# Recurrence mixer: two kinds of products interleaved, the gate chain cut into steps, order written out for each engine

## The chip, the cores and the metric

The kernel runs on one core of a Trainium2 chip. The metric is the device time of one execution in microseconds (us). The engines are named as the profile names them: PE is TensorE (PEld its weight loads), DVE is VectorE, ACT is ScalarE, POOL is GpSimd, SP is SyncE, whose queue issues most transfers.

## The reference, cut to what matters

The program is a stack of mixers and feed-forward networks over 512 tokens of width 1024, in eight stages. The change is in the third, the recurrence mixer (`rglru_mixer`), 1280 wide in ten heads of 128:

```python
proj = u @ w_in + b_in
ybr = jax.nn.gelu(proj[..., :LRU_WIDTH])
xbr = causal_dwconv(proj[..., LRU_WIDTH:], conv_w, conv_b)      # 4 taps
xh = xbr.reshape(bsz, s, LRU_HEADS, LRU_BLOCK)
gx = jax.nn.sigmoid(einsum('bshi,hij->bshj', xh, w_gx) + b_gx)
ga = jax.nn.sigmoid(einsum('bshi,hij->bshj', xh, w_ga) + b_ga)
log_a = LRU_C * ga * jax.nn.log_sigmoid(lam)
a_t = jnp.exp(log_a)
b_t = jnp.sqrt(-jnp.expm1(2.0 * log_a)) * gx * xbr
_, h = lax.associative_scan(_linear_combine, (a_t, b_t), axis=1)   # h_t = a_t h_(t-1) + b_t
out = (h * ybr) @ w_out + b_out
```

So a head has a branch product with a convolution behind it, two gate products of 128 by 128, a scan along the tokens, and a gelu product that multiplies the scan's result. `log_sigmoid(lam)` depends on the parameters alone.

## The kernel before, in words

Channels lie on the partitions, the 512 tokens (`T`) along a row. All matmuls are split in two parts of a value: a high part, rounded, and a low part, the remainder. A product of the input with a chunk of 128 output channels (`proj`) is 8 blocks of the contraction, each three matmuls of 512 columns (`mm3`: high by high, L429; low activation, L430; low weight, L431), so 24 in all, in one PSUM bank of the ring `mm`, which has three banks.

**Weights.** All weight chunks lie in one array in the order in which the program wants them. SP loads them two chunks at a time into `raw`. A chunk is split as two halves of 512 columns (`Weights._half`): the high part by a cast (`wh<-raw`), then the low part by a subtraction on VectorE (`wl<-raw`, L295). A plan says where the cast runs: "av" puts it on ScalarE (L292), "vv" on VectorE (L294). The plan is ("av",) in all stages but this one, where halves alternate by `PLAN = {"lru": ("av", "vv")}`. `W.next` splits ahead of need by `look`, two halves; `W.reserve` and `W.more` put halves into other tiles of the stage and split them earlier still.

**The stage.** At its entry `lru` computes what depends on the parameters alone: softplus of `lam` (17 steps on VectorE, one exp on ScalarE), the vector for the convolution's first columns (`less`) and halved gate biases (`hb`). Then a small scheduler, `Flow`, runs generators by priority and writes instructions in the order in which they yield. The generator `dense` makes the ten branch products b0 to b9 first. Behind each stand the convolution (`conv`: a first step on ScalarE, L690, three on VectorE, L693, and a correction) and the split of its result (`xb`). For each pair of heads it spawns `gates` with a delay: four gate products of three matmuls, four tanh from PSUM (L1051), two tanh (L1058), two exps (L1063), two square roots (L1066), and for each head a scan step of three VectorE instructions on `th`, `gt` and `h` (L1067 to L1070). The ten gelu products g0 to g9 follow: gelu on ScalarE, times `h`, split into `hs`. They come in groups of 4, 2 and 4, and each group's down product (`down`, 8 steps of one PSUM bank each, summed by VectorE into `acc`) is made behind the products of the next group. The last down product belongs to `stage_end`, with the norms of the next stage's input. Exp, square root and gelu (tanh shares gelu's and exp's) want different sets of ScalarE's function tables; where a set is wanted that isn't there, the program holds an `ACT_TABLE_LOAD`.

**What sets the order.** Within one engine a tile scheduler issues what the program writes, in its written order but for what its own priorities move forward; between engines semaphores hold.

Of the kernel before, what the change touches and what calls it, by code (L numbers as in the profile page):

```python
# [16 lines left out]
P = 128  # L17
# [68 lines left out]
G_MLA = _groups(4, 2, 2)  # L86
G_FF = {FF1: _groups(*(4,) * 8), FF2: _groups(*(4,) * 5, 2)}
# [74 lines left out]
def weights(i, used):  # L162
# [12 lines left out]
    lin = _up(w, list(range(10, 20)) + list(range(10)))  # L175
# [168 lines left out]
def build(tc, nc, aps, at, stages):  # L344
# [4 lines left out]
    with ExitStack() as st:  # L349
# [380 lines left out]
        def ssd(pl, ent, pre, fin):  # L730
# [213 lines left out]
            def last_homes():  # L944
                def two(a, b, bufs):
                    return lambda: tuple(pl.tile([P, T], F32R, name=n, tag=t, bufs=m)
                                         for n, t, m in (("wh", a, bufs[0]), ("wl", b, bufs[1])))

                def both():
                    t = pl.tile([P, 2, T], F32R, name="w2", tag="xdt", bufs=2)  # L950
# [54 lines left out]


        def lru(pl, ent, pre, fin):
            acc = [pl.tile([P, 1024], F32, name=f"acc{q}") for q in range(4)]
            NH = 10
            xs = ent.xs  # L1010
            flow = Flow()
            pre = list(pre)
            held_b = [None]


            few_ = pl.tile([P, 5 * NH], F32, name="few_")
# [6 lines left out]
            less = pl.tile([P, NH, 3], F32, name="less")  # L1023
# [9 lines left out]
            hseq, held, done = {}, [None], [0]  # L1033

            def unit():
# [6 lines left out]
            def gates(pair, xb, xbs):  # L1042
                hold = []
                for h in pair:
                    if h % 4 == 0:
                        held[0] = W.next("lg")
                    for n in range(2):
                        ps = mmps("ax")
                        mm3(ps, held[0].blk(2 * (h % 4) + n), xbs[h], True, True)
                        gt = tmp("gt")  # L1050
                        A.activation(gt, ps, AF.Tanh, scale=0.5, bias=hb[:, NH * n + h:NH * n + h + 1])  # L1051
                        hold.append(gt)
                gx, ga = hold[0::2], hold[1::2]

                ths, ats = [], []
                for n, h in enumerate(pair):
                    th = tmp("th")
                    A.activation(th, ga[n], AF.Tanh, scale=psp[:, h:h + 1], bias=psp[:, h:h + 1])  # L1058
                    V.scalar_tensor_tensor(gx[n], gx[n], 1.0, xb[h], op0=ALU.add, op1=ALU.mult)
                    ths.append(th)  # L1060
                for n, h in enumerate(pair):
                    a_ = tmp("at")
                    A.activation(a_, ga[n], AF.Exp, scale=nsp[:, h:h + 1], bias=nsp[:, h:h + 1])  # L1063
                    ats.append(a_)
                for n, h in enumerate(pair):
                    A.activation(ths[n], ths[n], AF.Sqrt, scale=0.25)  # L1066
                    V.scalar_tensor_tensor(ths[n], ats[n], 1.0, ths[n], op0=ALU.add, op1=ALU.mult)  # L1067
                    tt(gx[n], gx[n], ths[n])
                    hh = pl.tile([P, T], F32, name=f"h{h}")
                    V.tensor_tensor_scan(hh, ats[n], gx[n], initial=0.0, op0=ALU.mult, op1=ALU.add)  # L1070
                    hseq[h] = hh
                done[0] += 1
                yield 2.6, 0.0

            def dense():
                for p in range(0, NH, 2):
                    xb, xbs = {}, {}
                    yield 0.0, 0.0, lambda: done[0] >= p // 2 - 1
                    for h in (p, p + 1):
                        ps = unit()  # L1080
                        o = conv("co", ps, 4, [vc("lcw", NH * t_ + h) for t_ in range(4)], lcb[:, h:h + 1])
                        tt(o[:, :3], o[:, :3], less[:, h], ALU.subtract)
                        xb[h], xbs[h] = o, split(pl, o, "xb", bufs=4)
                        yield 5.2, 0.0
                    flow.spawn(gates((p, p + 1), xb, xbs), 0, 11.0)
                prev = None
                for q, grp in enumerate(G_LRU):
                    hs = []
                    if q == 1:
                        held_b[0] = row(5)  # L1090
                    for h in grp:
                        ps = unit()
                        t = tmp("t")
                        A.activation(t, ps, AF.Gelu_apprx_tanh, bias=vc("lbin", h))
                        yield 5.2, 0.0, lambda: h in hseq
                        tt(t, t, hseq[h])
                        hs.append(split(pl, t, "hs", bufs=7))
                    if q == 2:
                        W.reserve(len(W.used) + len(prev), last_homes())
                    if prev is not None:  # L1100
                        for d in down("lout", prev, acc, bias_first if q == 1 else None):
                            if q == 2:
                                W.more()
                            yield d
                    prev = hs
                held[0] = prev

            def last_homes():
                def hp(h):
                    return lambda: tuple(pl.tile([P, T], F32R, name=n, tag=f"h{h + e}")  # L1110
                                         for e, n in enumerate(("wh", "wl")))

                def xb():
                    return tuple(pl.tile([P, T], F32R, name="w" + n, tag="xb" + n, bufs=4) for n in "hl")
                return [xb, xb, xb, xb, hp(0), hp(2), hp(4)]

            def bias_first(a, ps, h):
                tt(a, ps, held_b[0][h], ALU.add)
            flow.spawn(dense(), 3)
            flow.run()  # L1120
            return fin("lout", held[0], acc, 1)
# [674 lines left out]
        def ffn(pl, ent, pre, fin, n, side=None):  # L1796
# [39 lines left out]
            def last_homes():  # L1836
                def one(k):
                    def f():
                        if n == 1 and k < 2:
                            t = pl.tile([P, 2, T], F32R, name="w2", tag=("HD", "W_")[k], bufs=1)  # L1840
                        else:
                            t = pl.tile([P, 2, T], F32R, name=f"w2{k}")
# [28 lines left out]
        PLAN = {"lru": ("av", "vv")}  # L1871
# [62 lines left out]
```

## Time and profile before

| | before |
|---|---|
| median of 3 runs (lowest, highest) | 2921.78 us (2921.23, 2925.98) |
| profiled execution | 2921.57 us, its span 2919.8 us |
| PE busy | 2849.1 us, 98% of the span |
| PEld busy | 2328.5 us, 80% |
| DVE busy | 1845.0 us, 63% |
| ACT busy | 1285.7 us, 44% |
| POOL busy | 314.3 us, 11% |
| mean granted clock of TensorE | 0.991 |
| instructions, bytes moved by DMA | 35383, 285.70 MB |

The table gives averages over eight stages with different loads. The recurrence stage's own products run from 1000.35 to 1165.12 us of the span. A row of the order views below gives the start in us, the length of one, the engine, the line, the operation with its output and inputs, and in brackets the idle time before it and whose result ended it; x4 is four in a row of the same kind, whose time is the sum. Granted clock is the share of full clock that TensorE was given.

### The profile page before, as it was taken

How to read it: one execution, taken by the hardware profiler on the slowest of the kernel's cores; microseconds unless marked ns; L12 is line 12 of the kernel's file. 1: busy time of each engine (PE TensorE's matmuls, PEld its weight loads, DVE VectorE, ACT ScalarE, POOL GpSimd, SP SyncE). 2: the span in 40 equal slices, each digit the busy share in tenths (PEclk: the TensorE clock that was granted, in tenths of full speed). 3: DMA queues.
4: the chain of work that ended last, by engine and by line, in shares of the span. 5: the costliest groups of instructions: out<-in, count | busy, mean ns of one | idle time of the engine just before them, and what ended most of it. 6: DMA issues, size and time to landing. Idle time of an engine off the chain costs nothing.

```text
span 2919.8 us, 35383 instructions
## 1 busy us (share of the span) xinstructions
PE 2849.1 (98%) x13528; PEld 2328.5 (80%) x13528; DVE 1845.0 (63%) x3001; ACT 1285.7 (44%) x2273; POOL 314.3 (11%) x458
## 2 busy tenths in 40 slices
PE   8999999999999989999999999999999999999998
PEld 7777778888888867888878878888888876788886
DVE  6887776556556777775766665655445566554454
ACT  5444346434334672643433354654333454443332
POOL 1233210000000000112233221100000000000000
PEclk9999999999999989999999999999999999999999
DMA  3212222222223123133333336522222221122222
GB/s 138 73 58 73 76 105 87 101 87 101 101 87 126 55 79 137 62 105 109 130 109 121 122 127 190 156 70 101 101 87 101 91 73 44 58 101 101 87 100 81
DMA packets 100184, 285.70 MB, mean 98 GB/s; under 512 B 19632, under 2 KB 28336, under 8 KB 99504
## 3 DMA queue, kind: packets, MB, share of 16 engines
q1 hardware_dynamic: 89376, 272.15, 26.8%
q10 hardware_dynamic: 10640, 11.30, 1.2%
q8 instruction: 106, 1.74, 0.2%
q14 instruction: 62, 0.51, 0.1%
HBM read 269.31 MB, written 14.12 MB: 97 GB/s over the span
## 4 chain that ended last, share of the span: by engine, by line
PE 76%; DVE 4%; ACT 3%; issue 1%; POOL 1%; DMA 0%; DVEq 0%; POOLq 0%; ACTq 0%
PE mm L429 16%; PE mm L430 16%; PE mm L431 16%; PE dn L561 6%; PE dn L560 6%; PE dn L562 6%; PE mm L562 1%; PE mm L560 1%; PE mm L561 1%; PE ax L1744 1%; PE ax L1766 1%; ACT sq L506 1%; DVE wl L295 1%; PE ax L1743 1%; DVE x L425 1%
## 5 line engine op out<-in xcount | busy, mean ns | idle before, releaser
L292 ACT CAST wh<-raw 128x512 fp32r<-128x512 f32 x889 | 548.9, 622 | 1135.3 <-PE mm L430 719.0
L429 PE MATMUL mm<-xh,wh 128*128 128x512 f32 (+1 forms) x2600 | 980.7, 379 | 21.3 <-DVE xl L549 11.8
L295 DVE TENSOR_TENSOR wl<-raw,wh 128x512 fp32r<-128x512 f32 x922 | 667.7, 731 | 511.1 <-ACT wh L292 495.0
L431 PE MATMUL mm<-xh,wl 128*128 128x512 f32 (+1 forms) x2600 | 977.9, 377 | 10.9 <-DVE wl L295 10.8
L430 PE MATMUL mm<-xl,wh 128*128 128x512 f32 (+1 forms) x2600 | 977.9, 377 | 1.3 <-DVE xl L549 0.9
L429 PEld LDWEIGHTS mm<-xh,wh 128*128 128x128 f32 x2600 | 491.5, 190 | 117.9 <-DVE xl L549 13.0
L431 PEld LDWEIGHTS mm<-xh,wl 128*128 128x128 f32 x2600 | 493.2, 190 | 100.9 <-DVE wl L295 12.8
L430 PEld LDWEIGHTS mm<-xl,wh 128*128 128x128 f32 x2600 | 493.2, 190 | 89.4 <-DVE xl L549 2.3
L560 PE MATMUL dn<-wh,hsh 128*128 128x512 f32 x816 | 321.1, 394 | 2.6 <-DVE acc L425 2.6
L561 PE MATMUL dn<-wl,hsh 128*128 128x512 f32 x816 | 322.2, 395 | 0.2 <-DVE wl L295 0.2
L562 PE MATMUL dn<-wh,hsl 128*128 128x512 f32 x816 | 317.5, 389 | 0.0
L514 POOL TENSOR_SCALAR rr<-ss 128x1 f32<-128x1 f32 x52 | 15.9, 306 | 1689.8 <-ACT sq L506 1688.8
L560 PEld LDWEIGHTS dn<-wh,hsh 128*128 128x128 f32 x816 | 153.4, 188 | 38.9 <-DVE acc L425 3.0
L562 PEld LDWEIGHTS dn<-wh,hsl 128*128 128x128 f32 x816 | 153.6, 188 | 34.3
L561 PEld LDWEIGHTS dn<-wl,hsh 128*128 128x128 f32 x816 | 153.8, 189 | 31.2 <-DVE wl L295 0.7
L693 DVE SCALAR_TENSOR_TENSOR ca<-mm,vec,ca 128x510 f32<-128x510 f32 x216 | 161.6, 748 | 11.8 <-ACT ca L690 8.2
L425 DVE TENSOR_TENSOR acc<-dn,acc 128x512 f32<-128x512 f32 x112 | 76.9, 687 | 88.5 <-PE dn L562 88.1
L425 DVE TENSOR_TENSOR x<-dn,x 128x512 f32<-128x512 f32 x96 | 66.0, 689 | 103.9 <-PE dn L562 103.9
L693 DVE SCALAR_TENSOR_TENSOR cb<-mm,vec,cb 128x510 f32<-128x510 f32 (+1 forms) x128 | 95.7, 748 | 10.7 <-ACT cb L690 8.7
L443 ACT CAST hsh<-act 128x512 fp32r<-128x512 f32 x108 | 67.2, 622 | 69.1 <-DVE act L425 69.0
L425 DVE TENSOR_TENSOR hsl<-act,hsh 128x512 fp32r<-128x512 f32 x108 | 79.8, 739 | 10.6 <-ACT hsh L443 2.7
L690 ACT ACTIVATE ca<-mm,vec 128x512 f32<-128x512 f32 x108 | 83.8, 776 | 5.6 <-PE mm L431 5.3
(504 smaller groups left out, 3191.3 us busy)
## 6 DMA issues: line engine op xcount, KB each, us to landing
raw<-w SPq DMA_DIRECT2D x233, 1024.0 KB, 4.8
sD<-s5t SPq DMA_DIRECT2D x4, 1024.0 KB, 6.9
row<-rows SPq DMA_DIRECT2D x12, 256.0 KB, 5.2
sR<-s5t SPq DMA_DIRECT2D x4, 768.0 KB, 4.3
x<-x SPq DMA_DIRECT2D x8, 256.0 KB, 5.1
xo<-x ACTq DMA_DIRECT2D x8, 256.0 KB, 4.8
s5t<-el ACTq DMA_DIRECT2D x8, 256.0 KB, 2.9
s5t<-HD ACTq DMA_DIRECT2D x4, 512.0 KB, 3.1
```

Of the source, the lines that this page charges most:

```text
L292: c.nc.scalar.copy(hi, r)
L295: (c.nc.gpsimd if e[1] == "g" else c.nc.vector).tensor_tensor(lo, r, hi.bitcast(F32), op=ALU.subtract)
L425: (eng or V).tensor_tensor(o, a, b, op=op)
L429: PE.matmul(ps, lhsT=wh, rhs=xh, start=first, stop=False)
L430: PE.matmul(ps, lhsT=wh, rhs=xl, start=False, stop=False)
L431: PE.matmul(ps, lhsT=wl, rhs=xh, start=False, stop=last)
L443: A.copy(hi, src)
L560: PE.matmul(ps, lhsT=hh[:, qs], rhs=wh, start=first, stop=False)
L561: PE.matmul(ps, lhsT=hh[:, qs], rhs=wl, start=False, stop=False)
L562: PE.matmul(ps, lhsT=hl[:, qs], rhs=wh, start=False, stop=last)
L690: A.activation(o, src, AF.Identity, scale=w[nt - 1], bias=b)
L693: V.scalar_tensor_tensor(o[:, d:], src[:, :T - d], w[j], o[:, d:], op0=ALU.mult, op1=ALU.add)
```

## The change

The stage is no longer run by `Flow`; it is written out.

- **Products interleaved.** `LRU_UNITS` lists branch (b) and gelu (g) products in the order b0 to b5, g0, g1, b6, b7, g2, g3, b8, b9, g4 to g9, and the weights are stored in that order.
- **The gate chain as steps.** A class `Gates` holds a pair of heads. `first` (a head's two gate products), `second` (its three tanh) and `third` (a VectorE product) are written into the code of a later product, one head for each product; `exps`, `roots` (two square roots, and then a preload of gelu's table set) and `scan` stand between products. The last pair's gate products stand inside the first down product.
- **Order fixed.** `in_order` adds, for PE, ACT, DVE and Pool, a dependence of each instruction on the one written before it on the same engine, so that the scheduler moves nothing.
- **Weights.** `PLAN` is empty: all casts run on ScalarE. In all, 33 casts leave VectorE for ScalarE. For three gate chunks the second half gets tiles of its own (`W.homes`).
- **Parameters.** Softplus, `less` and `hb` move into `lru_vectors`, which the feed-forward stage ahead calls at its fourth group; their tiles live in the pool `main`.
- **Tiles.** The convolution's output `cb` has four buffers, the scan's result `hq` four in place of ten tiles `h0` to `h9`, `hs` six for seven. The two transfers of the output bias stand at the stage's start and not at the second group.
- Table loads: 52 in the program where 46 stood, 16 where 11 stood in the recurrence stage. The renaming of `w2` to `wh2` in other stages changes nothing else.

```diff
+LRU_UNITS = [(u[0], int(u[1])) for u in
+             "b0 b1 b2 b3 b4 b5 g0 g1 b6 b7 g2 g3 b8 b9 g4 g5 g6 g7 g8 g9".split()]
...
-    lin = _up(w, list(range(10, 20)) + list(range(10)))
+    lin = _up(w, [10 * (b == "b") + h for b, h in LRU_UNITS])
...
+        class in_order:
+            def __enter__(self):
+                self.n = len(nc.cur_bb.bb.instructions)
+            def __exit__(self, *a):
+                last = {}
+                E = mybir.EngineType
+                for i in nc.cur_bb.bb.instructions[self.n:]:
+                    if i.engine not in (E.PE, E.Activation, E.DVE, E.Pool):
+                        continue
+                    if i.engine in last:
+                        tc.add_manual_dep(i, last[i.engine].name, mybir.DependencyInfo(
+                            mybir.DependencyClass.NoSync, mybir.DependencyReason.DATA), reason="in order")
+                    last[i.engine] = i
...
+            for n in (1, 9, 19):
+                W.homes[2 * (len(W.used) + n) + 1] = lambda: tuple(
+                    pl.tile([P, T], F32R, name=m, tag=m + "x") for m in ("wh", "wl"))
...
+                def second(self, n):
+                    h = self.hs[n]
+                    gs = []
+                    for m in range(2):
+                        gt = tmp("gt")
+                        A.activation(gt, self.ps[m], AF.Tanh, scale=0.5, bias=hb[:, NH * m + h:NH * m + h + 1])
+                        gs.append(gt)
+                    self.g[n] = gs
+                    th = tmp("th")
+                    A.activation(th, gs[1], AF.Tanh, scale=psp[:, h:h + 1], bias=psp[:, h:h + 1])
...
+                def roots(self):
                     for n in range(2):
...
+                        A.activation(self.th[n], self.th[n], AF.Sqrt, scale=0.25)
+                    table("gelu_apprx_tanh_and_others")
...
+            def unit(first=None):
+                kind, h = units.pop(0)
+                ps = product()
+                if first:
+                    gs[first[0]].first(first[1])
...
+            with in_order():
+                unit(), unit(), unit()
+                unit((0, 0))
+                unit((0, 1))
+                g0.exps(), g0.roots()
+                unit()
+                g0.scan(0)
+                unit((1, 0))
+                g0.scan(1)
+                unit((1, 1))
+                g1.exps()
+                unit()
+                g1.roots()
+                unit()
+                g1.scan(0)
+                unit((2, 0))
...
+                downs(grp[0], bias_first, {0: (g3.exps,), 1: (g3.roots,), 2: (lambda: g3.scan(0),),
+                                           3: (lambda: g3.scan(1),), 4: (lambda: gate(0),), 6: (lambda: gate(1),)})
+                unit()
+                g4.exps()
+                unit()
+                g4.roots(), g4.scan(0)
+                W.reserve(len(W.used) + 2 + 2, last_homes())
+                downs(grp[1], None, {1: (lambda: g4.scan(1),), 7: (W.more,)})
+                unit(), W.more(2)
+                unit(), W.more(2)
...
+                if n == 0 and q == 3:
+                    lru_vectors()
...
-        PLAN = {"lru": ("av", "vv")}
+        PLAN = {}
```

Where the instructions stand is read from the built programs. First ScalarE, before, at the second pair of heads: `gt`, `th` and `at` are the gates' tiles, `xbh` the high part of a convolution's result `co`, `wh` the high part of a weight.

```order
L1058 ACTIVATE th<-gt,few__8367 128x512 x2
L1063 ACTIVATE at<-gt,few__8367 128x512 x2
L443 CAST xbh<-co 128x512
L1066 ACT_TABLE_LOAD
L1066 ACTIVATE th<-th 128x512 x2
L292 CAST wh<-raw 128x512
L690 ACTIVATE co<-mm,few__8367,vec 128x512
L292 CAST wh<-raw 128x512 x2
```

After, ScalarE at the first pair, from the convolution of b4 to the first weight cast behind the gate chain (`cb` is the convolution's tile now):

```order
L1146 ACTIVATE cb<-mm,few__5776,vec 128x512
L1104 ACTIVATE gt<-ax,few__5776 128x512 x2
L1109 ACTIVATE th<-gt,few__5776 128x512
L446 CAST xbh<-cb 128x512
L1119 ACT_TABLE_LOAD
L1119 ACTIVATE at<-gt,few__5776 128x512 x2
L1124 ACT_TABLE_LOAD
L1124 ACTIVATE th<-th 128x512 x2
L1077 ACT_TABLE_LOAD
L295 CAST wh<-raw 128x512 x2
```

The exps, the square roots and three table loads stand in a row, ahead of the two casts that the next product's weights need; before, one load stood there.

Second, VectorE at the second down product (the sums `acc` of heads 4 and 5), before. `h_9099` is a scan's result, `hsl` the low part of its product with a gelu.

```order
L425 TENSOR_TENSOR t<-t,h_9099 128x512
L425 TENSOR_TENSOR acc_8363<-mm,acc_8363 128x512
L295 TENSOR_TENSOR wl<-raw,wh 128x512
L425 TENSOR_TENSOR hsl<-t,hsh 128x512
L425 TENSOR_TENSOR acc_8364<-mm,acc_8364 128x512
L295 TENSOR_TENSOR wl<-raw,wh 128x512
L425 TENSOR_TENSOR acc_8365<-mm,acc_8365 128x512
L295 TENSOR_TENSOR wl<-raw,wh 128x512
L425 TENSOR_TENSOR acc_8366<-mm,acc_8366 128x512
L294 CAST wh<-raw 128x512
L425 TENSOR_TENSOR acc_8363<-mm,acc_8363 128x512
```

After, the same place, with the last pair's scan steps (`th`, `gt`, `hq`) between:

```order
L428 TENSOR_TENSOR t<-t,hq 128x512
L428 TENSOR_TENSOR hsl<-t,hsh 128x512
L1130 SCALAR_TENSOR_TENSOR th<-at,th 128x512
L428 TENSOR_TENSOR gt<-gt,th 128x512
L1133 SCALAR_TENSOR_TENSOR hq<-at,gt 128x512
L298 TENSOR_TENSOR wl<-raw,wh 128x512 x2
L428 TENSOR_TENSOR acc_8395<-mm,acc_8395 128x512
L428 TENSOR_TENSOR acc_8396<-mm,acc_8396 128x512
L1130 SCALAR_TENSOR_TENSOR th<-at,th 128x512
L428 TENSOR_TENSOR gt<-gt,th 128x512
L1133 SCALAR_TENSOR_TENSOR hq<-at,gt 128x512
L428 TENSOR_TENSOR acc_8397<-mm,acc_8397 128x512
```

A scan step and two low parts of weights stand ahead of the first sum, and a second scan step between the second and the third; before, the sums alternated with low parts and no scan stood there.

## Rows read from the trace of the kernel before

**Rows 1.** Busy time by stretch: length, PE, PEld, DVE, ACT, POOL, clock, DMA

```profile
1000.35:1165.12 164.77, 147.75 (x613) 118.42 (x614) 123.86 (x211) 86.23 (x129) 0.00 (x0) 0.94 0.29 104
750.00:915.00 165.00, 165.00 (x727) 136.28 (x726) 97.53 (x141) 64.11 (x103) 0.00 (x0) 1.00 0.28 96
```

**Rows 2.** Waits of PE, recurrence stage: waiter, releaser, us in sum, times, longest

```profile
PE mm L431 <- DVE wl L295: 10.8, 3, 3.6
PE mm L429 <- ACT wh L292: 6.1, 2, 3.4
```

**Rows 3.** TensorE in order of time: start, us, instruction, [idle before it, releaser]

```profile
419.27 0.50 PE L560 MATMUL ax<-wh,hsh 128*128 128x512 f32 x1 [3.04 <-ACT hsh L443]
...
1019.63 0.40 PE L429 MATMUL ax<-xbh,wh 128*128 128x512 f32 x1
...
1022.44 0.40 PE L429 MATMUL mm<-xh,wh 128*128 128x512 f32 x1
...
1027.69 0.39 PE L431 MATMUL mm<-xh,wl 128*128 128x512 f32 x1
...
1057.97 0.80 PE L431 MATMUL mm<-xh,wl 128*128 128x512 f32 x1 [3.60 <-DVE wl L295]
1058.57 0.63 PE L429 MATMUL mm<-xh,wh 128*128 128x512 f32 x1
...
1063.25 0.39 PE L431 MATMUL mm<-xh,wl 128*128 128x512 f32 x1
...
1502.82 0.50 PE L560 MATMUL dn<-wh,hsh 128*128 128x512 f32 x1 [2.57 <-DVE acc L425]
...
1503.66 0.63 PE L560 MATMUL dn<-wh,hsh 128*128 128x512 f32 x1
...
1507.03 0.40 PE L562 MATMUL dn<-wh,hsl 128*128 128x512 f32 x1
```

**Rows 4.** ScalarE in order of time, first pair of heads, same columns

```profile
1007.13 2.47 ACT L1051 ACTIVATE gt<-ax,few__8367 128x512 f32<-128x512 f32 x4
1009.50 1.51 ACT L1058 ACTIVATE th<-gt,few__8367 128x512 f32<-128x512 f32 x2
1010.91 0.81 ACT L1063 ACTIVATE at<-gt,few__8367 128x512 f32<-128x512 f32 x1
1011.62 0.61 ACT L443 CAST xbh<-co 128x512 fp32r<-128x512 f32 x1
1012.13 0.81 ACT L1063 ACTIVATE at<-gt,few__8367 128x512 f32<-128x512 f32 x1
1012.97 1.28 ACT L1066 ACT_TABLE_LOAD   x1
1014.26 1.16 ACT L1066 ACTIVATE th<-th 128x512 f32<-128x512 f32 x2
1015.32 0.76 ACT L690 ACTIVATE co<-mm,few__8367,vec 128x512 f32<-128x512 f32 x1
1015.98 0.61 ACT L292 CAST wh<-raw 128x512 fp32r<-128x512 f32 x1
```

**Rows 5.** VectorE in order of time behind it, same columns

```profile
1014.92 1.29 DVE L1067 SCALAR_TENSOR_TENSOR th<-at,th 128x512 f32<-128x512 f32 x2 [1.97 <-ACT th L1066]
...
1017.34 2.33 DVE L1070 TENSOR_TENSOR_SCAN h<-at,gt 128x512 f32<-128x512 f32 x2
1019.59 0.72 DVE L693 SCALAR_TENSOR_TENSOR co<-mm,vec,co 128x509 f32<-128x509 f32 x1
1020.23 0.68 DVE L295 TENSOR_TENSOR wl<-raw,wh 128x512 fp32r<-128x512 f32 x1
```

**Rows 6.** TensorE in order of time, the stage's entry, same columns

```profile
991.02 0.39 PE L430 MATMUL mm<-xl,wh 128*128 128x256 f32 x1 [0.86 <-DVE xl L549]
...
1000.35 0.47 PE L429 MATMUL mm<-xh,wh 128*128 128x512 f32 x1 [0.52 <-DVE co L693]
```

**Rows 7.** The SP queue in order of time, the bias rows, same columns

```profile
1086.68 0.89 SPq L413 DMA_DIRECT2D row<-rows  x2
```

More of the change, by code (lines that the diff above doesn't have):

```diff
@@ L1040, in unit, with table @@
                 return ps
-            def gates(pair, xb, xbs):
-                hold = []
-                for h in pair:
+            def table(name):
+                before = [i for i in nc.cur_bb.bb.instructions[-400:]
+                          if i.engine == mybir.EngineType.Activation and i.opcode == "Activation"]
+                load = A.preload_act_table_set(name)
+                tc.add_manual_dep(load.ins, before[-1].name, mybir.DependencyInfo(
+                    mybir.DependencyClass.NoSync, mybir.DependencyReason.DATA), reason="table in order")
@@ L1045, in gates, with __init__, first @@
+            class Gates:
+                def __init__(self, p):
+                    self.hs = (2 * p, 2 * p + 1)
+                    self.g, self.th, self.at = {}, {}, {}
+                def first(self, n):
+                    h = self.hs[n]
                     if h % 4 == 0:
                         held[0] = W.next("lg")
-                    for n in range(2):
[L1048 to L1064, printed above, removed]
@@ L1075, in dense @@
[L1075 to L1106, printed above, removed]
@@ new lines, in scan @@
+                def scan(self, n):
+                    h = self.hs[n]
+                    th, at, gx = self.th[n], self.at[n], self.g[n][0]
+                    V.scalar_tensor_tensor(th, at, 1.0, th, op0=ALU.add, op1=ALU.mult)
+                    tt(gx, gx, th)
+                    hh = pl.tile([P, T], F32, name="hq", tag="hq", bufs=4)
+                    V.tensor_tensor_scan(hh, at, gx, initial=0.0, op0=ALU.mult, op1=ALU.add)
+                    hseq[h] = hh
+            gs = [Gates(p) for p in range(5)]
@@ new lines, in downs, with bias_first @@
+            def downs(grp, first, steps):
+                for n, _ in enumerate(down("lout", [hsp[h] for h in grp], acc, first)):
+                    for f in steps.get(n, ()):
+                        f()
+            held_b = [pl.tile([P, T], F32, name=f"row{h}") for h in range(2)]
+            for h in range(2):
+                nc.sync.dma_start(held_b[h], aps["rows"][5:6, h * T:h * T + T].to_broadcast([P, T]))
+            def bias_first(a, ps, h):
+                tt(a, ps, held_b[h], ALU.add)
@@ L1108, in last_homes, with two, part @@
             def last_homes():
[L1109 to L1113, printed above, removed]
+                def two(t, m):
+                    return lambda: tuple(pl.tile([P, T], F32R, name=n, tag=t, bufs=m) for n in ("wh", "wl"))
+                def part():
                     return tuple(pl.tile([P, T], F32R, name="w" + n, tag="xb" + n, bufs=4) for n in "hl")
-                return [xb, xb, xb, xb, hp(0), hp(2), hp(4)]
@@ L1117, in bias_first, with gate @@
[L1117 to L1121, printed above, removed]
+                return [two("cb", 4), two("cb", 4), part, part, part, part, two("hq", 4)]
+            g0, g1, g2, g3, g4 = gs
+            with in_order():
[14 more added lines that the diff above has]
+                unit((2, 0))
+                g1.scan(1)
+                unit((2, 1))
+                g2.exps()
+                unit()
+                g2.roots()
+                unit()
+                g2.scan(0)
+                unit((3, 0))
+                g2.scan(1)
+                unit((3, 1))
+                grp = [[hsp_ for hsp_ in g] for g in G_LRU]
+                def gate(n):
+                    g4.first(n), g4.second(n), g4.third(n)
+                downs(grp[0], bias_first, {0: (g3.exps,), 1: (g3.roots,), 2: (lambda: g3.scan(0),),
+                                           3: (lambda: g3.scan(1),), 4: (lambda: gate(0),), 6: (lambda: gate(1),)})
+                unit()
+                g4.exps()
+                unit()
+                g4.roots(), g4.scan(0)
[3 more added lines that the diff above has]
+                unit(), W.more(2)
@@ L1124, in build @@
+            return fin("lout", [hsp[h] for h in grp[2]], acc, 1)
         TWOPI = 2.0 * np.pi
```

77 lines of the change are left out of this document (56 added, 21 removed).

## The prediction

> **What bounds the kernel now.** I began with busy time by stretch. In the recurrence stage TensorE gets 613 matmuls done in 164.77 us at a mean granted clock of 0.94, while 165 us of the feed-forward stage ahead of it hold 727 at 1.00 [rows 1]. VectorE (123.86 us busy) and ScalarE (86.23 us) have room on average [rows 1], so no engine is full: the loss is waiting. The waits of TensorE in that stretch come next: 10.8 us in three for the low part of a weight (`wl`), 6.1 us in two for its rounded high part (`wh`) [rows 2]. Third, TensorE in order of time. A product is 24 matmuls at 0.228 us (1022.44 to 1027.69 holds 23), 5.48 us; the gates of two heads are twelve in 2.81 us, 1.40 a head [rows 3]. [...]
>
> At full pace the stretch is 17 products (93.2 us), ten heads of gates (14.0) and 144 down matmuls at 0.23 (33.1), 140.3 in sum; 24.5 us are waits and slow clock. That is all the change can win there, plus 1.4 us of two waits at the stage's entry (0.86 and 0.52 us) [rows 6].
>
> The last two views are ScalarE and VectorE in order of time, which price every step from start to start. ScalarE: gate tanh 0.59, second tanh 0.70, exp 0.71, square root 0.53, table load 1.28, cast 0.51 (lands after 0.62), conv's first step 0.66 [rows 4]. VectorE: scan step (three instructions) 2.33 a head, conv step 0.64, low part 0.60 (lands after 0.68) [rows 5].
>
> **The change part by part.** Removed: softplus at the entry. Its VectorE steps stand ahead of the `xl` that TensorE waits for, so I count both waits of [rows 6] as won, 1.4 us. It moves into the feed-forward stage with two table loads. TensorE has cover there (727 in 165 us), so I take 0; the bound is 2.57, the wait of a later feed-forward stage behind VectorE work [rows 3]. The two bias-row transfers go up the SP queue past seven weight loads; they hold it for 0.89 us [rows 7], and the load behind them cannot start before a weight buffer is free, so I take 0 and bound it by that 0.89.
>
> Moved: 33 weight casts from VectorE to ScalarE, 0.51 each. Added: table loads, 16 in the stage where 11 stood. A load by itself takes 1.28 us; the next ScalarE instruction starts 0.01 later, and the load starts 0.03 after the exp before it ends [rows 4]. [...]
>
> Work per pair of heads fits: on ScalarE 2 x 1.17 (conv, cast), 2 x 1.10, 4 x 0.59, 2 x 0.70, 2 x 0.71, 2 x 0.53, 3 x 1.29 and 9 x 0.51, some 19.3 us; TensorE needs 4 x 5.48 + 2.8 = 24.7. But each engine now keeps the written order, and I follow the order the change shows. The products are called b0 to b9 and g0 to g9.
>
> *First pair*, from the end of b4 as 0. TensorE: gates to 1.40, b5 to 6.88, then g0. ScalarE: second gate's tanh from 1.55, second tanh done 3.1, cast of b4 (behind three conv steps of VectorE) 3.7, exp load 5.0, two exps 6.5, square root load 7.8, two roots 8.95, gelu load 10.25; only then the weight cast for g0, 10.87. TensorE waits 4.0, and 0.2 more for the low part; 0.2 at the first gates. Sum 4.4.
>
> *Two middle pairs*, from the end of g1 (later g3). ScalarE: cast of g1's product 3.5, exp load and two exps 6.2, casts for b7 7.2: TensorE waits 0.2. Conv of b6 from 7.2: VectorE is free at 8.05 and done at 10.1, cast 10.8, square root load, two roots, gelu load 14.55, cast for g2 15.15. TensorE ended b7 at 12.6: it waits 2.55, then 0.2. Once, VectorE's conv of b7 (18.4), cast, low part (19.7) and scan step (22.05) stand ahead of the gate weight's low part (22.7), wanted at 21.3: 1.4. Sum 2 x 2.95 + 1.5 = 7.4.
>
> *First down product*, from the end of g5. Four casts follow g5's own at 3.5; the second weight chunk's high part lands at 4.1, its low part at 5.45, wanted at 2.8: waits of 1.3 and 1.15. Exps, roots and gelu load then run to 12.4; VectorE has three sums and two scan steps (to 18.35) ahead of the fourth chunk's low part (19.05), wanted at 16.7: 2.35. Sum 4.8.
>
> *Second down product*, from the end of g6, where it turns from weights to PSUM. Cast 2.1, exp load and exps 4.8, two casts 5.85, gelu load 7.15, gelu of g7 7.85, its product 8.5 and cast 9.2, square root load 10.5, first root 11.15, second 11.7, gelu load 13.05, next cast 13.65. VectorE does a scan step (13.5) and two low parts (14.9) before the first sum, landing at 15.6. TensorE starts at 5.5, waits 0.5 for a low part, has filled the three `mm` banks at 10.1 and waits for that sum: 5.5; 0.7 at a later step. Sum 6.7.
>
> *Last down product*, from the end of g9: the second chunk's casts stand behind g9's cast (2.05), high part 2.65, low part 4.0, wanted at 1.4: 1.25 and 1.1. VectorE has low parts between its norm steps (0 to 1.2): 0.6. Sum 2.95.
>
> These waits come to 26.25 us. Slow clock: two exceed 4 us, like the one that cost 2.2; I take 1.9 and, where the later 0.7 swallows a part, 1.2. Five lie near 2.5. Of the two rows near them, 2.57 was followed by eight slow matmuls (1503.66 to 1507.03, 1.55 lost) and 3.04 by none [rows 3]; half would be 2.5 times, and one falls into the gate wait, so 1.5 x 1.55 = 2.3. Sum 5.4.
>
> After: 26.25 + 5.4 = 31.65 in place of 24.5 + 1.4 = 25.9: **5.75 us more**. The profiled execution is 2921.57 us, 1.77 above its span and 0.2 under the median, so 2927.3, and by the median 2927.5.
>
> The bounds of this case: waits 15% shorter (22.3) with slow clock after the two long ones alone (3.1) give 25.4, 0.5 less than before, 2921.2; slow clock after all seven (3.1 + 5 x 1.55) gives 37.1, 11.2 more, 2932.9.
>
> **The rivals.** *The interleave covers its chains (faster).* If VectorE and ScalarE reach the middle pairs and the last product ahead of my times, those waits go: 4.4 + 4.8 + 6.7 + 3.1 = 19.0 against 25.9, 2914.9; were all gone, 2895.9. For it: both engines' sums fit. Against: the casts stand behind three loads in a fixed order, whatever the averages. It decides where the cast for g2 lands by 12.6 rather than 15.15. I give 0.12.
>
> *The shorter waits leave the clock alone (no change).* The chains hold, none of the five near 2.5 us slows TensorE, as the 3.04 one did not [rows 3]: 26.25 + 3.1 - 25.9, 3.5 more, 2925.3; with the waits a little shorter, none more. This is the lower half of my own case; 0.38.
>
> *Every switch of set drains ScalarE (slower by far).* If each of some fourteen loads on these chains held ScalarE for as long again as the load takes (1.28 [rows 4]), the time would be 18 us higher, 2945. The row has no such gap: 0.02. [...]
>
> *The order is not kept.* The built program shows each engine's instructions as written; under 0.01, in the first rival.
>
> **How the numbers follow.** A measurement of this kernel can tell about 0.2%, 5.8 us, from no change, and my forecast lies at that edge. Its upper half, over 2927.6, has 0.48, the lower half 0.38, the covering 0.12, the drain 0.02: slower 0.50, same 0.38, faster 0.12. Waits that I overlooked can only add; chains that I stretched can only take away. The range leaves out one tenth at either end: 2917, inside the covering rival, to 2935, past the bound of 2932.9.
>
> **What would show it.** [...] If no wait for `wh` tops 2 us, the covering rival is right and I am wrong; if the load is followed by a gap, the drain. If TensorE waits in the feed-forward stage ahead, softplus is not hidden.

## The result, and the profile after

The changed kernel takes 2986.65 us (median of 4 runs, 2984.11 to 2989.70) against 2922.28 for the kernel before: a ratio of 1.0218, 95% interval 1.0201 to 1.0236. It is slower by 64 us. The direction was forecast, the size was not: 2927.5, with 2935.0 as the upper end. All ratios compare fast runs; two of the ten runs of b_const below were slow (3700 and 7100 us), which lifts its median by 1 us.

First the page of the kernel after: the span, TensorE's busy time, and the group of the first matmul of every product (count, busy time, mean ns of one, idle time before them).

```profile
span 2988.0 us, 35386 instructions
...
PE 2912.3 (97%) x13528; PEld 2339.6 (78%) x13528; DVE 1840.0 (62%) x2968; ACT 1313.2 (44%) x2312; POOL 317.4 (11%) x458
...
L432 PE MATMUL mm<-xh,wh 128*128 128x512 f32 (+1 forms) x2600 | 996.4, 385 | 24.2 <-DVE xl L569 12.5
```

The number of matmuls is the one of before, 13528, and TensorE is busy 63 us longer (2849.1 before). Idle time can't do that; slower matmuls can. The second view, busy time by stretch, says where; columns as in [rows 1].

```profile
750.00:915.00 165.00, 165.00 (x707) 133.04 (x707) 94.20 (x137) 58.41 (x94) 0.00 (x0) 1.00 0.27 93
...
1019.59:1202.43 182.84, 158.27 (x620) 122.05 (x619) 115.74 (x176) 109.25 (x161) 0.00 (x0) 0.93 0.23 78
```

The first row is the feed-forward stage, which the change hardly touches. It is full, at a granted clock of 1.00, as before, and yet holds 707 matmuls in 165 us where 727 stood [rows 1]. The matmuls themselves are slower, and they are so in every stage. The trace gives the pace: from start to start, where TensorE didn't wait, a product's 512-column matmul takes 0.2342 us on average (6490 in the trace), and 0.2271 before (6505).

The second row is the recurrence stage, from its first own product to the last down product: 182.8 us, 164.8 before [rows 1]. TensorE's waits in and behind it (waiter, releaser, us in sum, times, longest), to be held against [rows 2]:

```profile
PE mm L432 <- ACT wh L295: 9.7, 3, 4.3
PE mm L580 <- DVE acc L428: 5.4, 1, 5.4
PE mm L581 <- DVE wl L298: 3.9, 3, 2.8
PE mm L432 <- DVE xl L569: 2.2, 1, 2.2
PE ax L432 <- ACT wh L295: 2.8, 1, 2.8
...
PE ax L580 <- ACT wh L295: 1.3, 1, 1.3
PE mm L580 <- ACT wh L295: 1.3, 1, 1.3
```

These are the waits that the forecast named, but for one: the 2.8 us for the gates' weights (`ax`, L432). So there are two losses to tell apart: a pace, everywhere, which the forecast doesn't have at all, and the stage's own chains.

### The profile page after: what moved, and what is told of

It is laid out like the page before. It is cut to its first block, busy times and chain, and to the rows that moved or that the text cites. A ratio compares the mean times of both kernels' runs of the same rounds, so it can differ in the third digit from the quotient of the medians.

```text
span 2988.0 us, 35386 instructions
## 1 busy us (share of the span) xinstructions
PE 2912.3 (97%) x13528; PEld 2339.6 (78%) x13528; DVE 1840.0 (62%) x2968; ACT 1313.2 (44%) x2312; POOL 317.4 (11%) x458
## 4 chain that ended last, share of the span: by engine, by line
PE 77%; DVE 4%; ACT 3%; issue 1%; POOL 1%; DMA 0%; DVEq 0%; POOLq 0%; ACTq 0%
PE mm L432 16%; PE mm L433 16%; PE mm L434 16%; PE dn L580 6%; PE dn L582 6%; PE dn L581 6%; PE mm L580 1%; PE mm L582 1%; PE mm L581 1%; PE ax L1850 1%; DVE wl L298 1%; PE ax L1872 1%; PE ax L1849 1%; ACT sq L526 1%; DVE cb L1151 1%
## 5 line engine op out<-in xcount | busy, mean ns | idle before, releaser
L295 ACT CAST wh<-raw 128x512 fp32r<-128x512 f32 x936 | 572.7, 620 | 1154.9 <-PE mm L433 754.6
L432 PE MATMUL mm<-xh,wh 128*128 128x512 f32 (+1 forms) x2600 | 996.4, 385 | 24.2 <-DVE xl L569 12.5
L433 PE MATMUL mm<-xl,wh 128*128 128x512 f32 (+1 forms) x2600 | 994.1, 383 | 0.4
L434 PE MATMUL mm<-xh,wl 128*128 128x512 f32 (+1 forms) x2600 | 993.4, 382 | 0.0
L432 PEld LDWEIGHTS mm<-xh,wh 128*128 128x128 f32 x2600 | 493.4, 190 | 134.7 <-DVE xl L569 13.7
L580 PE MATMUL dn<-wh,hsh 128*128 128x512 f32 x864 | 341.6, 395 | 2.6 <-DVE acc L428 2.6
L582 PE MATMUL dn<-wh,hsl 128*128 128x512 f32 x864 | 340.7, 394 | 0.0
L580 PEld LDWEIGHTS dn<-wh,hsh 128*128 128x128 f32 x864 | 163.0, 189 | 39.3 <-DVE acc L428 3.0
L582 PEld LDWEIGHTS dn<-wh,hsl 128*128 128x128 f32 x864 | 162.9, 189 | 36.7
```

The costliest lines, as they stand in the source:

```text
L295: c.nc.scalar.copy(hi, r)
L432: PE.matmul(ps, lhsT=wh, rhs=xh, start=first, stop=False)
L433: PE.matmul(ps, lhsT=wh, rhs=xl, start=False, stop=False)
L434: PE.matmul(ps, lhsT=wl, rhs=xh, start=False, stop=last)
L580: PE.matmul(ps, lhsT=hh[:, qs], rhs=wh, start=first, stop=False)
L582: PE.matmul(ps, lhsT=hl[:, qs], rhs=wh, start=False, stop=last)
```

## The experiments

### Is it the place of the tiles?

The one part of the change that reaches every stage adds no instruction: the small tiles `few_` and `less` now lie in the pool `main`. They take 352 bytes there, so all that lies behind (`wh` and `wl`, the temporaries, the stages' tiles) starts 352 bytes later in each partition, while the activations `xh` and `xl`, ahead of them, stay. **b_main** does that alone, in the kernel before:

```diff
-            few_ = pl.tile([P, 5 * NH], F32, name="few_")
+            few_ = main.tile([P, 5 * NH], F32, name="few_")
...
-            less = pl.tile([P, NH, 3], F32, name="less")
+            less = main.tile([P, NH, 3], F32, name="less")
```

> The kernel before, with one edit: its two small tiles few_ and less are taken from the pool main and no longer from the stage's pool, as the change does. Not one instruction is added or moved; every tile that lies behind main (raw, wh, wl, S, the temporaries, the stages' pools) starts 352 bytes later, so 32 bytes off a multiple of 64, while the activations xh and xl stay. Theory A (place in memory): a matmul is slower when its two operands start at different offsets within 64 bytes; 6758 more of the 512-column matmuls come to be so, at the 0.0065 us that the traces of before and after show between the two kinds (0.2277 and 0.2342), 44 us, and 4 to 7 for the down products: 2970 to 2974 us. Theory B (the loss of pace comes with the change's instructions: casts on ScalarE, table loads, fixed order): 2922 us, as before.

Measured: 2969.91, ratio 1.0155 (1.0138 to 1.0172), 47 us more, with every instruction as before. Theory A holds, at the lower end of its range, and B falls. In the same stretch as above:

```profile
750.00:915.00 165.00, 165.00 (x712) 133.72 (x711) 94.18 (x137) 57.95 (x93) 0.00 (x0) 1.00 0.26 92
```

**b_const** takes both tiles from `const` (the same two lines, with `const.tile`), which lies ahead of the activations, so activations and weights move together.

> The kernel before, with the same two tiles taken from the pool const, which lies ahead of main. Now the activations xh and xl start 352 bytes later too, as the weights do: nearly all operands lie 32 off a multiple of 64, but both of a matmul alike. Theory A with the difference of the two operands as the cause: 2920 to 2924 us, as before. Theory A with each operand's own offset as the cause: 2970 us or more. Theory B: 2922.

Measured: 2924.33, ratio 1.0000 (0.9990 to 1.0010). For these products the operands' own place doesn't matter, their difference does:

```profile
750.00:915.00 165.00, 165.00 (x727) 136.24 (x726) 96.27 (x140) 61.73 (x99) 0.00 (x0) 1.00 0.29 100
```

**b_less** (the second of the two lines alone, with `main.tile`) and **a_pack** (the changed kernel, the two tiles as one of 320 bytes) were to show that 64 bytes are the size that counts.

> The kernel before, with the tile less alone taken from main: the tiles behind main start 128 bytes later, still at multiples of 64, but no longer at the same offset within 512 bytes as the activations. Theory A, with 64 bytes as the size that counts: 2920 to 2924 us. If a size of 256 or 512 bytes counts: 7000 matmuls at 0.002 to 0.0065 more, 2936 to 2968 us. Theory B: 2922.

> The changed kernel, with few_ and less as one tile of 320 bytes in main and not as two of 224 and 128: the tiles behind main start 320 bytes later than in the kernel before, at multiples of 64 again; no instruction changes. Theory A: the loss of pace goes, and what is left is the recurrence stage's own chains, some 6 us of waits and 7 of slow clock more than before: 2933 to 2937 us, up to 2944 if 128 bytes count for a little. Theory B: 2987 us, as after.

```diff
-            few_ = main.tile([P, 5 * NH], F32, name="few_")
+            both_ = main.tile([P, 8 * NH], F32, name="few_")
+            few_ = both_[:, :5 * NH]
...
-            less = main.tile([P, NH, 3], F32, name="less")
+            less = both_[:, 5 * NH:].rearrange("p (h e) -> p h e", e=3)
```

Measured: b_less 2961.14 (1.0129, 1.0114 to 1.0144), a_pack 2980.01 (1.0191, 1.0175 to 1.0206). My rule of 64 bytes fell; both differences are multiples of 64 and cost most of what 352 does. The row of b_less:

```profile
750.00:915.00 165.00, 165.00 (x713) 133.66 (x713) 94.33 (x137) 60.02 (x97) 0.00 (x0) 1.00 0.28 96
```

**b_ones** moves the activations 512 bytes forward, by giving the tile `ones` a pool behind `main`:

```diff
         rpool = pool("rpool")
+        late = pool("late")
...
-        ones = const.tile([P, P], F32, name="ones")
+        ones = late.tile([P, P], F32, name="ones")
```

> The kernel before, with the tile ones (512 bytes) in a pool of its own behind main and not in const: the activations start 512 bytes earlier, the weights stay. If the difference counts within 512 bytes or less: 2920 to 2925 us. If it counts within 1024 or 2048 bytes (all large tiles are 2048 long): 6500 products at some 0.006 more, 2955 to 2970 us.

Measured: 2921.71, ratio 0.9996 (0.9987 to 1.0005). So a shift by 512 bytes costs nothing, and the difference counts within 512 bytes or a part of that (b_less leaves 256 open):

| weights' start less activations' start, within 512 bytes | kernels | mean start to start of a product's matmul, us (count in a trace) |
|---|---|---|
| 0 | before, b_const, b_ones, a_const | 0.2271 (6489 to 6505) |
| 128 | b_less | 0.2327 (6506) |
| 320 | a_pack | 0.2333 (6495) |
| 352 | after, b_main | 0.2342 (6490, 6501) |

In these products the weights are the operand that PEld loads (`lhsT`, 128x128) and the activations the other one (128x512), so the table gives the loaded one's start less the other's. A difference of 256 was in no run for the products. One small group of another stage had it: `mm<-wh,kvngh`, whose operands lie 256 bytes apart in before, 64 in b_small and 0 in b_best, takes 0.2274, 0.2333 and 0.2278 us there (43 pairs in each trace). That speaks for 256 as the size that counts, by few matmuls.

The kernel before had this luck in its products, but not everywhere. Its down products in the feed-forward stages, where the activations are the loaded operand, have operands 192 bytes apart within 512, at 0.2289 us (2563). **b_small** puts them together:

```diff
+        small = pool("small", bufs=3)
         const = pool("const")
...
-        small = pool("small", bufs=3)
         wk = pool("wk", bufs=12)
```

> The kernel before, with the pool small (192 bytes) opened first and not between the weights' tiles and the temporaries: the weights' tiles and the feed-forward stages' tiles hsh and hsl come to lie at the same offset within 2048 bytes (they were 1856 apart), and activations and weights stay alike. If the difference sets the pace, the 2448 matmuls of the feed-forward's down products go from the 0.2290 us that the trace of before shows to the 0.2271 of the up products: 4.5 us less, 2916 to 2920. If not: 2922.

Measured: the down matmuls go to 0.2269 us (2564), and the time to 2919.07, ratio 0.9990 (0.9981 to 0.9999): the pace as expected, the time 3 us less where 4.5 was worked out. **b_best** does that and, for what is left, moves or widens six small tiles (`few_`, `less`, `cwh`, `sbg`, `s32`, `rt`):

> The kernel before, its instructions unchanged, with all large tiles at one place within 512 bytes: the pool small first, few_ and less in const, and four small tiles of other stages widened (cwh, sbg, s32, rt), so that nearly every matmul's two operands start alike. Over b_small (2919.1) some 690 matmuls at 0.0025 to 0.006 are won, 2 to 4 us: 2914 to 2918. If the place of the operands counts only for the large groups of products: 2919.

```diff
-            few_ = pl.tile([P, 5 * NH], F32, name="few_")
+            few_ = const.tile([P, 5 * NH], F32, name="few_")
...
-            cwh = pl.tile([P, 5 * NT], F32, name="cwh")
+            cwh = pl.tile([P, 5 * NT + 8], F32, name="cwh")[:, :5 * NT]
...
-            hng, sbg = sm("hng", 4), sm("sbg", 4)
+            hng, sbg = sm("hng", 4), sm("sbg", 80)[:, :4]
```

Measured: 2915.19, ratio 0.9969 (0.9959 to 0.9980): the kernel before, its instructions unchanged, faster by 0.3%.

For the down products the difference isn't all. In after it is 192 as well, and yet they ran at 0.2333 us from 500 to 950 us of its span, where b_main has 0.2289 at the same difference. What decides there is open; over the 576 matmuls that the trace shows there it is 2.5 us.

### The stage's own loss

**a_const** is the changed kernel with both tiles in `const`, so the pace is the old one.

> The changed kernel, with few_ and less in the pool const, ahead of the activations: xh, xl, wh and wl all start 352 bytes later, so that their difference is the one of the kernel before. No instruction changes. If the difference of the two operands' places sets the pace of all products, that loss is gone, and what is left is the recurrence stage's own: 6.3 us more of waits and 6.7 of slow clock in its main stretch, and the move of tiles by itself (2924.3 measured): 2934 to 2939 us. If part of the pace is lost to the change's instructions: above 2945.

Measured: 2937.37, ratio 1.0053 (1.0040 to 1.0065), and 0.2271 us a matmul (6489). The place is 49 us of the 64, the stage's chains 15. **a_ahead** puts, in a_const, the casts that TensorE waits for ahead of the gate chain:

```diff
-                g0.exps(), g0.roots()
+                W.more(2), g0.exps(), g0.roots()
...
-                g1.exps()
+                W.more(2), g1.exps()
                 unit()
-                g1.roots()
+                W.more(2), g1.roots()
...
```

> The kernel of the run before (changed kernel, tiles in const), with one edit: at the first three pairs the two weight casts that stood behind the exps, and behind the square roots and table loads, are written ahead of them on ScalarE. Theory: the waits of 4.3 and twice 2.7 us before g0, g2 and g4 come from the fixed place of those casts, and with each goes the slow clock that followed it (about 2.2 us each): 16 us less than the run before, 2919 to 2924 us. Rival: ScalarE's whole chain is late, and the waits only turn up at the next chunk: within 4 us of the run before.

Measured: 2941.85, ratio 1.0065 (1.0052 to 1.0078): the rival, at 4.5 us over a_const where it allowed 4. The three waits went, and others came at the next chunk; TensorE's waits in this stage now:

```profile
PE ax L432 <- ACT wh L295: 5.6, 2, 2.8
PE mm L580 <- DVE acc L428: 5.4, 1, 5.4
PE mm L434 <- DVE wl L298: 4.8, 2, 2.6
PE mm L432 <- ACT wh L295: 3.9, 2, 2.6
```

**a_scan** takes, in a_const again, the largest single wait, by moving the sums and two casts ahead of the last pair's scan steps:

```diff
-                g4.roots(), g4.scan(0)
+                W.more(2), g4.roots()
...
-                downs(grp[1], None, {1: (lambda: g4.scan(1),), 7: (W.more,)})
+                downs(grp[1], None, {3: (lambda: g4.scan(0),), 5: (lambda: g4.scan(1),), 7: (W.more,)})
```

> The same kernel a_const; in the second down product the four sums and the next chunk's two casts are written ahead of the last pair's scan steps, and of its square roots. The wait of 5.4 us for a sum and the slow clock behind it (1.7 to 2.8) come from the scan step that stands ahead: 7 to 8 us less, 2929 to 2931. If the wait turns up at a later step: 2934 or more.

Measured: 2935.13, ratio 1.0036 (1.0024 to 1.0049). The 5.4 us became two waits of 2.5 in sum; the gain over a_const is 2 us by the medians and 5 by the ratios, under the 7 to 8 expected. The time lies where the other answer put it, the wait at a later step:

```profile
PE mm L580 <- DVE acc L428: 2.5, 2, 1.5
```

**a_plan** undoes another part in a_const: alternate casts go back to VectorE.

```diff
-        PLAN = {}
+        PLAN = {"lru": ("av", "vv")}
```

> The same kernel a_const with one part of the change undone: alternate weight casts of the stage are on VectorE again. If it is ScalarE's added work (17 us of casts) that makes the waits: 2926 to 2932 us. If it is the place of a cast in the written order, on whichever engine, the first half of every chunk still stands behind the loads, the waits of 2.8 and 4.4 us stay, and VectorE is later: 2935 to 2945.

Measured: 2946.22, ratio 1.0071 (1.0059 to 1.0084). ScalarE's added casts are not the cause. **a_free** takes the fixed order of a_const away, on all four engines that had it, and leaves all else that is written, casts included:

```diff
-            with in_order():
+            if True:
```

> The changed kernel with its two tiles in const (a_const, 2937.4 us), without the dependences of in_order: the tile scheduler may move instructions again, and on VectorE it writes low parts of weights ahead of convolution steps and both scan steps of a pair in a row. Theory: the fixed order makes ScalarE and VectorE wait for each other step by step (three convolutions at 3.94 us each at the stage's start, 2.64 of it idle on ScalarE), so the stage's waits fall back to those of the kernel before: 2921 to 2928 us. Rival: the chains are as long in any order, and the order is not the cause: 2934 to 2940.

Measured: 2900.66, ratio 0.9915 (0.9902 to 0.9929): 37 us less than a_const, well under what either theory said, and 0.85% faster than the kernel before. The stage's stretch, and all that is left of TensorE's waits in it:

```profile
999.01:1144.12 145.11, 143.00 (x623) 116.42 (x623) 113.63 (x181) 118.80 (x171) 0.00 (x0) 1.00 0.31 108
```

```profile
PE mm L581 <- DVE wl L298: 1.3, 2, 1.0
PE ax L580 <- ACT hsh L446: 0.7, 1, 0.7
PE mm L432 <- DVE cb L1151: 0.5, 1, 0.5
PE mm L580 <- DVE acc L428: 0.2, 1, 0.2
```

The granted clock is 1.00, and 145.1 us stand near the 140.3 that the prediction gave as full pace. ScalarE works more than in after (118.8 us for 109.3), since the scheduler's order holds more table loads (25 in the stage at 1.28 us, 16 in a_const). It doesn't matter: casts of weights stand between the loads, ahead of need. ScalarE at the first pair:

```profile
1008.37 1.28 ACT L1124 ACT_TABLE_LOAD   x1
1009.66 0.63 ACT L1124 ACTIVATE th<-th 128x512 f32<-128x512 f32 x1
1010.20 0.60 ACT L446 CAST xbh<-cb 128x512 fp32r<-128x512 f32 x1
1010.71 1.30 ACT L295 CAST wh<-raw 128x512 fp32r<-128x512 f32 x2
1011.91 0.77 ACT L1146 ACTIVATE cb<-mm,few__5776,vec 128x512 f32<-128x512 f32 x1
1012.70 1.28 ACT L1104 ACT_TABLE_LOAD   x1
```

Which engine's order is it? **o_act** and **o_dve** keep the written order on one engine alone, with the tiles in `const` (o_dve has `E.DVE` there):

```diff
-                    if i.engine not in (E.PE, E.Activation, E.DVE, E.Pool):
+                    if i.engine not in (E.Activation,):
```

> The changed kernel with its tiles in const, and the dependences of in_order on ScalarE alone; VectorE, TensorE and Pool may be reordered. If it is ScalarE's fixed order that makes the waits (casts of weights behind loads, and behind a cast that waits for VectorE): 2928 to 2938 us, near a_const's 2937.4. If VectorE's: 2899 to 2908, near a_free's 2900.7.

> The same with the dependences on VectorE alone. If VectorE's fixed order makes the waits (convolution steps and scan steps ahead of the low parts of weights): 2928 to 2938 us. If ScalarE's: 2899 to 2908. If the two wait for each other in turn, so that either alone holds both: both runs above 2920.

Measured: o_act 2926.17 (1.0014, 1.0005 to 1.0023), o_dve 2918.47 (0.9985, 0.9976 to 0.9993). None of the three answers came true; the third wanted both runs above 2920. ScalarE's order alone costs 26 us over a_free, VectorE's alone 18, and the order of all four engines 37. Each brings its own kind of wait. ScalarE's:

```profile
PE mm L432 <- ACT wh L295: 7.9, 5, 2.8
...
PE ax L432 <- ACT wh L295: 2.9, 1, 2.9
```

VectorE's:

```profile
PE mm L580 <- DVE acc L428: 4.6, 1, 4.6
PE mm L434 <- DVE wl L298: 3.7, 4, 1.7
```

With one engine fixed the scheduler writes other orders on the rest, so this is no clean split; it shows that undoing VectorE's or ScalarE's order alone doesn't give the gain. TensorE's order was not tried by itself.

**f_main** undoes the fixed order in the changed kernel and leaves the tiles where the change put them; **f_best** joins the free order and the places of b_best.

> The changed kernel as it is, its two tiles in main, without the dependences of in_order: the one of its two costs undone alone. If the two costs add up: 2900.7 and the 46 to 49 us that the tiles' place cost (b_main over before 47, after over a_const 49): 2945 to 2951.

> a_free with the places of b_best: the changed kernel without its fixed order, and nearly all matmuls' operands at one place within 512 bytes. If the two gains add up: 2900.7 less the 8 to 9 us of b_best, 2891 to 2895 us.

Measured: f_main 2947.04 (1.0084, 1.0069 to 1.0100), 46.4 us over a_free: the two costs add up. f_best 2893.36, ratio 0.9903 (0.9889 to 0.9916), 30 us under the kernel before (2923.28 beside it) and 93 under the changed one: the fastest version. From its page:

```profile
span 2891.8 us, 35389 instructions
```

## Why the prediction was right or wrong

**The step that failed: what the change moves.** I went through instructions, queues and waits, and took the move of `few_` and `less` as free. It changes where the weights lie against the activations, and that is 49 of the 64 us (after against a_const). The prediction has no term for it. No view of the profile before shows it, since there the products' operands start alike. A list of the tiles' places in both programs would have shown that nearly all tiles move by 352 bytes; that something slows single groups was to be seen before in the paces of matmuls of the same size, 0.2271 us in the products and 0.2289 in the down products. The prediction itself used 0.228 for a product's matmul and 1.40 us for the six of a head's gates, 0.234 each, and didn't ask why.

**The stage's chains.** Without the place the change costs 15.3 us (a_const), and the forecast had 5.75; 2937.37 would still lie above the upper end. So the direction came from the mechanism that was forecast, but only 15 of the 64 us did. Term by term, in the trace of after:

| wait of TensorE | forecast, us | measured, us |
|---|---|---|
| first gates | 0.2 | 2.75 |
| g0 | 4.0 | 4.27 |
| before b7, and at its place in the next pair | 0.2 each | none |
| g2 and g4 | 2.55 each | 2.72, 2.69 |
| low parts behind these three | 0.2 each | none |
| gate weight's low part, once | 1.4 (in the sum 1.5) | 0.2 |
| first down product | 1.3, 1.15, 2.35 | 1.26, 0.91, 2.76 |
| second down product | 0.5, 5.5, 0.7 | 0.23, 5.42, none |
| last down product | 1.25, 1.1, 0.6 | 1.29, 0.31, none |
| sum | 26.25 | 24.8 |
| slow clock behind them | 5.4 | 16.6 |

(The slow clock is what a matmul took over 0.23 us, where it took over 0.27 us.) With 41.4 in place of the 31.65 forecast the cost is 15.5 over 25.9, near the measured 15.3. That it comes so close is partly chance: the table is of after, the 15.3 of a_const.

*The chains held.* ScalarE at the first pair of after, which the forecast walked by durations of [rows 4]:

```profile
1041.31 1.28 ACT L1119 ACT_TABLE_LOAD   x1
1042.60 1.52 ACT L1119 ACTIVATE at<-gt,few__5776 128x512 f32<-128x512 f32 x2
1044.13 1.28 ACT L1124 ACT_TABLE_LOAD   x1
1045.42 1.15 ACT L1124 ACTIVATE th<-th 128x512 f32<-128x512 f32 x2
1046.59 1.28 ACT L1077 ACT_TABLE_LOAD   x1
1047.88 1.14 ACT L295 CAST wh<-raw 128x512 fp32r<-128x512 f32 x2
```

The next instruction starts 0.01 us behind the end of each of the three loads, so the rival in which a load holds ScalarE for as long again is out. VectorE at the second down product, where the sum that TensorE waits for (start 1179.16) stands behind a scan step and two low parts, as the order of the change says:

```profile
1175.38 0.69 DVE L1130 SCALAR_TENSOR_TENSOR th<-at,th 128x512 f32<-128x512 f32 x1 [1.25 <-ACT th L1124]
1176.11 0.69 DVE L428 TENSOR_TENSOR gt<-gt,th 128x512 f32<-128x512 f32 x1
1176.83 1.23 DVE L1133 TENSOR_TENSOR_SCAN hq<-at,gt 128x512 f32<-128x512 f32 x1
1177.97 1.27 DVE L298 TENSOR_TENSOR wl<-raw,wh 128x512 fp32r<-128x512 f32 x2
1179.16 1.28 DVE L428 TENSOR_TENSOR acc<-mm,acc 128x512 f32<-128x512 f32 x2
```

*The term that was mis-sized: the slow clock.* I priced five waits near 2.5 us at half of 1.55, after two rows of other stages [rows 3], and the two over 4 us at 1.9 and 1.2, below a 2.2. That 2.2 is eleven matmuls at 0.425 us, from 1058.57 to 1063.25 behind the wait of 3.60 [rows 3], held against 0.228; the granted clock there is 0.50. No run shows the 1.9 or the 1.2: in after, 2.3 us of slow clock followed the wait of 4.27 us and 1.5 the one of 5.42. Each of the six waits of 2.69 us and more was followed by 7 to 13 matmuls of over 0.27 us from start to start, most of them at 0.43 us and a granted clock of 0.50: 1.5 to 2.3 us lost each time. TensorE at g0:

```profile
1043.89 0.40 PE L434 MATMUL mm<-xh,wl 128*128 128x512 f32 x1
1048.55 0.80 PE L432 MATMUL mm<-xh,wh 128*128 128x512 f32 x1 [4.27 <-ACT wh L295]
1049.15 0.63 PE L433 MATMUL mm<-xl,wh 128*128 128x512 f32 x1
...
1052.56 0.63 PE L432 MATMUL mm<-xh,wh 128*128 128x512 f32 x1
```

The granted clock of that stretch is 0.50 (columns as in [rows 1]):

```profile
1049.15:1052.99 3.84, 3.84 (x11) 2.94 (x9) 3.00 (x6) 1.20 (x3) 0.00 (x0) 0.50 0.00 0
```

Length alone doesn't decide it: a wait of 3.04 us was followed by no matmul of 0.43 us, at a granted clock of 1.00, and one of 2.57 us by eight, at 0.51 [rows 3]; in a_const one of 2.76 us was followed by three of over 0.27 us. In this stage of the kernel before, three waits of 3.6 us were followed by 7 to 12 of over 0.27 us; behind those of 3.38 and 2.69 us only two matmuls ran before the next wait.

*The wait that I missed: the first gates.* I began the walk at the end of b4. The three products that the stage gets finished have their convolutions ahead, in a fixed order, and ScalarE and VectorE then wait for each other in turn: 3.94 us for each, 2.64 of it idle on ScalarE, and the four casts behind (the gates' weights among them) start at 1027.45.

```profile
1019.57 0.78 ACT L1146 ACTIVATE cb<-mm,few__5776,vec 128x512 f32<-128x512 f32 x1
1022.99 0.62 ACT L446 CAST xbh<-cb 128x512 fp32r<-128x512 f32 x1 [2.64 <-DVE cb L428]
1023.51 0.78 ACT L1146 ACTIVATE cb<-mm,few__5776,vec 128x512 f32<-128x512 f32 x1
1026.93 0.62 ACT L446 CAST xbh<-cb 128x512 fp32r<-128x512 f32 x1 [2.64 <-DVE cb L428]
1027.45 2.18 ACT L295 CAST wh<-raw 128x512 fp32r<-128x512 f32 x4
```

In these rows ScalarE idles 2.64 us at a cast that waits for VectorE, twice, and the casts of weights written behind it start only when it is done.

*The entry.* Both waits of [rows 6] are gone. Two others just ahead of them, 1.49 us for `xl` and 0.40 for `xh`, stand in both kernels; no wait came up in the feed-forward stage ahead. At the stage's other end the wait for `xl` is 2.17 us, where 1.49 stood; I had not counted that.

**The rivals.** The covering rival named the right condition, sums that fit, and gave 2914.9. In the change it is wrong, since the written order holds the casts back. Without that order (a_free) it is right, and more so: the interleave, the loads, all casts on ScalarE and the rest of the change together are 24 us faster than the kernel before (2924.81 beside it). I had taken the order as a given of the change and never priced it by itself; that one part costs 37 us. The rival of the shorter waits, in which the clock stays up, is out: the waits near 2.7 us lost 1.7 to 2.1 us of clock each.

What is open: how much each single place in the written order matters. a_ahead and a_scan mended places, and won nothing and 2 to 5 us; the waits moved on.

## What to carry to other kernels

A tile that is added or moved moves all tiles behind it (here by 352 bytes, which cost 47 us in b_main): compare the operands' addresses in both programs, and the pace of matmuls in a stretch without waits, before looking for waits. Where an order written by hand makes two engines wait for each other step by step, try the scheduler's order first; here mending single places twice moved the wait and won little. For a wait of some 3 us of TensorE allow for slow matmuls behind it and for none: the kernel before lost 2.5 us behind one of 3.60 us, and no matmul of 0.43 us followed one of 3.04 us.

## What the runs showed of the hardware

A 512-column matmul of these products takes 0.2271 us from start to start where its two operands start at the same offset within 512 bytes of a partition, and 0.2327 to 0.2342 at the differences of 128, 320 and 352 bytes that were run, up to 3%. For the products the pace belongs to the difference, not to either place (b_const, b_ones). A group of 43 at a difference of 256 took 0.2274, and down products at 192 took 0.2289 or, in part of after, 0.2333. In b_main, without a change to any instruction, a difference of 352 bytes cost 47 us. What makes a matmul slower there was not tried.
